# RMSNorm on one core: scaling shared between VectorE and GpSimd, squares on ScalarE, and a fixed instruction order

## The chip, the cores and the metric

The kernel runs on one core of one Trainium2 chip. The metric is the time on the device of one execution, in microseconds (us); a time quoted for a kernel is the median of its runs. The profiler's span of one execution is a little shorter than that time: 160.0 us for the kernel before, whose time in the same set of runs is about 162 us.

## The reference

The input is 16 x 1024 rows of 512 float32 values; gamma has 512 values.

```python
def reference(x, gamma):
    eps = 1e-5
    rms = np.sqrt(np.mean(x ** 2, axis=-1, keepdims=True) + eps)
    return (x / rms * gamma).astype(np.float32)
```

The work per row is a sum of squares, a root, a reciprocal and two multiplications. The input and the output are 33.55 MB each, so 67.1 MB have to be moved.

## The kernel before

The 16,384 rows are cut into four tiles of 128 partitions x 32 rows. Three buffers (slots) in SBUF, the core's memory for tiles, hold a tile each; rows are scaled in place and stored from there. Tile 3 goes into slot 0 again, so it can be loaded only after tile 0 has been stored. A "row" below is one row of 512 values on each of 128 partitions, so the core has 128 of them.

```python
def row_stats(slot, g):                      # 8 rows; gives 1/rms
    ...
    if (g // G) % 2:                         # every second group:
        for h in range(0, G, H):             # ScalarE squares 4 rows at once,
            nc.scalar.activation(out=sq, in_=slots[slot][:, g + h : g + h + H, :], func=AF.Square)
            nc.vector.tensor_reduce(...)     # VectorE sums them
    else:
        for r in range(G):                   # ScalarE squares and sums a row
            nc.scalar.activation(out=sq_scratch, ..., func=AF.Square, accum_out=ss[:, r : r + 1])
    nc.scalar.activation(out=rms, in_=ss, func=AF.Sqrt, ...)
    nc.vector.reciprocal(out=rstd, in_=rms)

def apply(slot, g, rstd):                    # VectorE scales all rows
    for r in range(G):
        nc.vector.scalar_tensor_tensor(..., scalar=rstd[:, r : r + 1], in1=gamma_b, ...)

def transfers(t, g):                         # all of them issued by SyncE, in this order
    if (t, g) == (0, 0):
        store(0, 0, 0, 1)                    # tile 0, slot 0, row 0
        load(1, 1, 0, 32)                    # all of tile 1
        load(2, 2, 0, 16)
        store(0, 0, 1, 2)
        load(2, 2, 16, 32)
    ...

ahead = row_stats(0, 0)
for k, (t, g) in enumerate(groups):
    rstd = ahead
    if k + 1 < len(groups):
        ahead = row_stats(slot_of[tn], gn)   # the next group's statistics,
    apply(slot_of[t], g, rstd)               # then this group's scaling
    transfers(t, g)
```

The loads of tiles 1 and 2 stand, in SyncE's order, behind the store of row 0. And although the program text has the next group's statistics ahead of this group's scaling, the order on each engine is chosen here by a scheduler.

## Time and profile before

| | before |
|---|---|
| time, median of 3 runs | 162.24 us (161.93 to 162.32) |
| span | 160.0 us |
| DMA queue q1, share of the span | 97.9% |
| VectorE busy | 122.6 us (77%) |
| ScalarE busy | 80.1 us (50%) |
| GpSimd busy | 0.2 us |

These are lines of the page of the kernel before. DVE is VectorE, ACT is ScalarE, POOL is GpSimd. The row DMA has one digit for each fortieth of the span (4 us): the busy share of the 16 DMA engines in tenths, 9 for 90% or more. The row GB/s has what they moved.

```profile
span 160.0 us, 409 instructions
...
PE 2.0 (1%) x2; PEld 0.5 (0%) x2; DVE 122.6 (77%) x163; ACT 80.1 (50%) x162; POOL 0.2 (0%) x4
...
DMA  5999999699699999997999999999996996999993
GB/s 197 524 393 393 430 487 508 279 524 491 295 395 396 456 467 434 494 461 323 445 393 475 426 410 426 475 410 410 491 524 295 508 491 295 467 434 410 426 475 147
...
q1 hardware_dynamic: 2160, 67.11, 97.9%
```

The DMA engines are busy from the first slice to the last, and no compute engine is. The windows view of the same kernel, with longer stretches, takes the jitter of the slices out. Its columns are the stretch, its length, the busy time and instructions of PE, PEld, DVE, ACT and POOL, the clock, the DMA share and GB/s. (A packet is counted where it is recorded, so a short stretch can show a little over 1.00.)

```profile
22.00:34.00 12.00, 0.00 (x0) 0.00 (x0) 9.23 (x8) 11.12 (x16) 0.00 (x0) 1.00 1.07 459
34.00:116.00 82.00, 0.00 (x0) 0.00 (x0) 76.61 (x105) 50.34 (x107) 0.00 (x0) 1.00 1.00 431
...
124.00:158.00 34.00, 0.00 (x0) 0.00 (x0) 22.59 (x32) 6.29 (x15) 0.00 (x0) 1.00 1.00 432
158.00:162.00 4.00, 0.00 (x0) 0.00 (x0) 0.00 (x0) 0.00 (x0) 0.00 (x0) 1.00 0.00 0
```

The queue moves 431 to 432 GB/s wherever it is full. The Trainium skill, "DMA: Bandwidth & Descriptors", section Specifications, gives a ceiling of 435 GB/s for the ports between the DMA engines and SBUF, and this trace, loads and stores together, agrees. So the kernel is bound by its transfers, and a faster compute engine has next to nothing to win.

The timeline of the kernel before around the first store has start, length, engine, line and operation. SPq is SyncE's sequencer, which issues the transfers.

```profile
15.55 0.20 DVE L83 RECIPROCAL rstd<-rms 128x8 f32<-128x8 f32 x1 [10.61 <-ACT rms L82]
15.79 3.40 DVE L88 SCALAR_TENSOR_TENSOR slot<-slot,rstd,gamma_b 128x512 f32<-128x512 f32 x5
16.57 0.35 SPq L45 DMA_DIRECT2D out_dram<-slot  x1
16.97 0.92 SPq L42 DMA_DIRECT2D slot<-in_x_dram  x2
```

VectorE scales row 0 straight after its reciprocal. The store goes out at 16.57 us and the loads of tiles 1 and 2 from 16.97 us, while tile 0 is still being loaded. These two groups of instructions give the cost of VectorE's work (busy us in total, mean ns of one):

```profile
L88 DVE SCALAR_TENSOR_TENSOR slot<-slot,rstd,gamma_b 128x512 f32<-128x512 f32 x128 | 85.8, 741 | 0.1
...
L71 DVE TENSOR_REDUCE ss<-sq 128x4 f32<-128x2048 f32 x16 | 35.9, 2277 | 3.6 <-ACT sq L70 3.6
```

### The profile page before, as it was taken

What the parts mean: (1) busy time and instruction counts of PE and PEld (TensorE: products, weight loads), DVE (VectorE), ACT (ScalarE), POOL (GpSimd) and SP (SyncE); (2) the same over time, 40 slices, a digit from 0 to 9 for tenths busy, and PEclk for the clock granted to TensorE, in tenths of its full rate; (3) what the DMA queues carried; (4) which work ended last, traced back from release to release, by engine and by line L of the source; (5) the groups of instructions that cost most, each with busy time, mean ns of one, the idle gap of its engine ahead of it and who ended that gap; (6) DMA issues with size and microseconds to landing.
All of it is one profiled execution on the core that took longest, in us unless ns stands there. A gap on an engine that the chain in (4) does not pass through costs nothing.

```text
span 160.0 us, 409 instructions
## 1 busy us (share of the span) xinstructions
PE 2.0 (1%) x2; PEld 0.5 (0%) x2; DVE 122.6 (77%) x163; ACT 80.1 (50%) x162; POOL 0.2 (0%) x4
## 2 busy tenths in 40 slices
PE   4000000000000000000000000000000000000000
PEld 1000000000000000000000000000000000000000
DVE  0101928999999509999999999999999999996000
ACT  3098029991291999996900960069709950000000
POOL 0000000000000000000000000000000000000000
DMA  5999999699699999997999999999996996999993
GB/s 197 524 393 393 430 487 508 279 524 491 295 395 396 456 467 434 494 461 323 445 393 475 426 410 426 475 410 410 491 524 295 508 491 295 467 434 410 426 475 147
DMA packets 2164, 67.13 MB, mean 420 GB/s; under 512 B 241, under 2 KB 241, under 8 KB 498
## 3 DMA queue, kind: packets, MB, share of 16 engines
q1 hardware_dynamic: 2160, 67.11, 97.9%
q14 instruction: 2, 0.02, 0.0%
q10 hardware_dynamic: 2, 0.00, 0.0%
HBM read 33.56 MB, written 33.55 MB: 419 GB/s over the span
## 4 chain that ended last, share of the span: by engine, by line
DVE 67%; DMA 14%; ACT 7%; issue 2%; DVEq 0%; SPq 0%
DVE slot L88 48%; DVE ss L71 18%; DMA slot<-in_x_dram 14%; ACT sq_scratch L76 3%; ACT sq L70 3%; DVE rstd L83 1%; ACT rms L82 1%; DVEq L155 0%; SPq L42 0%
## 5 line engine op out<-in xcount | busy, mean ns | idle before, releaser
L88 DVE SCALAR_TENSOR_TENSOR slot<-slot,rstd,gamma_b 128x512 f32<-128x512 f32 x128 | 85.8, 741 | 0.1
L76 ACT ACTIVATE sq_scratch<-slot 128x512 f32<-128x512 f32 x64 | 40.0, 625 | 10.0 <-DMA slot<-in_x_dram 8.7
L70 ACT ACTIVATE sq<-slot 128x2048 f32<-128x2048 f32 x16 | 29.8, 1865 | 18.8 <-DVE ss L71 11.5
L71 DVE TENSOR_REDUCE ss<-sq 128x4 f32<-128x2048 f32 x16 | 35.9, 2277 | 3.6 <-ACT sq L70 3.6
L82 ACT ACTIVATE rms<-ss,eps_t 128x8 f32<-128x8 f32 x16 | 4.6, 297 | 26.2 <-DVE ss L71 26.0
L83 DVE RECIPROCAL rstd<-rms 128x8 f32<-128x8 f32 x16 | 3.1, 196 | 16.3 <-ACT rms L82 16.3
L76 ACT ACTIVATION_READ_ACCUMULATOR sq_scratch<-slot 128x1 f32 x64 | 11.9, 186 | 0.0
L57 DVE COPY gamma_b<-sq 128x512 f32<-128x512 f32 x1 | 0.7, 691 | 3.3 <-PE sq L55 3.3
L55 PE MATMUL sq<-gamma_row,ones_col 1*128 1x512 f32 x2 | 2.0, 1122 | 2.2 <-DMA gamma_row<-in_gamma_dram 2.2
L76 ACT ACT_TABLE_LOAD x1 | 1.3, 1283 | 1.3 <-PEq L144 1.3
L82 ACT ACT_TABLE_LOAD x1 | 1.3, 1283 | 0.0
L53 DVE MEMSET ones_col<- 1x128 f32 x1 | 0.2, 165 | 0.8 <-PEq L144 0.8
L55 PEld LDWEIGHTS sq<-gamma_row,ones_col 1*128 1x128 f32 x2 | 0.5, 308 | 2.1 <-issue 2.1
L144 POOL MEMSET const-uint8-127<- 128x1 uint8 x1 | 0.1, 102 | 0.0
L144 POOL MEMSET const-bfloat16-1.0<- 128x1 bf16 x1 | 0.1, 101 | 0.0
L144 POOL MEMSET const-float32-0.0<- 128x1 f32 x1 | 0.1, 98 | 0.2 <-issue 0.2
L144 POOL MEMSET const-float32-1.0<- 128x1 f32 x1 | 0.1, 98 | 0.0
L60 DVE MEMSET eps_t<- 128x1 f32 x1 | 0.1, 59 | 0.0
## 6 DMA issues: line engine op xcount, KB each, us to landing
slot<-in_x_dram SPq DMA_DIRECT2D x4, 4096.0 KB, 32.1
out_dram<-slot SPq DMA_DIRECT2D x4, 4096.0 KB, 18.4
out_dram<-slot SPq DMA_DIRECT2D x1, 7680.0 KB
slot<-in_x_dram SPq DMA_DIRECT2D x1, 6144.0 KB, 21.6
slot<-in_x_dram SPq DMA_DIRECT2D x1, 2048.0 KB, 7.2
out_dram<-slot SPq DMA_DIRECT2D x2, 256.0 KB, 21.4
gamma_row<-in_gamma_dram ACTq DMA_DIRECT2D x1, 2.0 KB
slot<-in_x_dram SPq DMA_DIRECT2D x1, 25.9
```

Source lines behind the costliest of these rows:

```text
L53: nc.vector.memset(ones_col, 1.0)
L55: nc.tensor.matmul(gamma_psum[:, 0], ones_col, gamma_row, start=True, stop=True)
L57: nc.vector.tensor_copy(out=gamma_b, in_=gamma_psum[:, 0])
L60: nc.vector.memset(eps_t, eps)
L70: nc.scalar.activation(out=sq, in_=slots[slot][:, g + h : g + h + H, :], func=AF.Square)
L71: nc.vector.tensor_reduce(out=ss[:, h : h + H], in_=sq, axis=mybir.AxisListType.X, op=OP.add)
L76: nc.scalar.activation(out=sq_scratch, in_=slots[slot][:, g + r, :], func=AF.Square, accum_out=ss[:, r : r + 1],)
L82: nc.scalar.activation(out=rms, in_=ss, func=AF.Sqrt, bias=eps_t, scale=1.0 / D)
L83: nc.vector.reciprocal(out=rstd, in_=rms)
L88: nc.vector.scalar_tensor_tensor(out=slots[slot][:, g + r, :], in0=slots[slot][:, g + r, :], scalar=rstd[:, r : r + 1], in1=gamma_b, op0=O ...
L144: nc = _bacc.Bacc("TRN2", target_bir_lowering=False, num_devices=1)
```

## The change

The intent is to share the compute out better. ScalarE only squares, several rows at once. VectorE sums all rows, but scales only 80 of 128; GpSimd scales the other 48 in two passes, by 1/rms and by gamma. VectorE reads gamma from PSUM, the memory that a matmul writes to, and no longer from SBUF. The order is fixed as the program has it, VectorE's code is aligned (`addr_align(128)`), and the last tile is loaded ahead of the store of tile 1, the second one. The core of the diff:

```diff
+    ctx.enter_context(tc.manual_schedule())
+    nc.vector.addr_align(128, offset=0, max_nops=0)
...
+    groups = [                       # tile, first row, rows, pieces, GpSimd's rows
+        (0, 0, 8, (4, 4), 3),
+        (0, 8, 12, (7, 5), 5),
+        (0, 20, 12, (7, 5), 5),
+        (1, 0, 16, (7, 5, 4), 7),
...
+    def sum_squares(t, g, n, pieces, share):
...
+            nc.scalar.activation(out=sq[:, :m], in_=rows, func=AF.Square)
+            nc.vector.tensor_reduce(out=ss[:, r : r + m], in_=sq[:, :m], ...)
...
+    def scale_by_pool(rstd, t, g, n, pieces, share):
+        part = slots[slot_of[t]][:, g + n - share : g + n, :]
+        by_row = rstd[:, n - share : n].to_broadcast([P, share, D])
+        nc.gpsimd.tensor_tensor(out=part, in0=part, in1=by_row, op=OP.mult)
+        nc.gpsimd.tensor_tensor(out=part, in0=part, in1=gamma_b.to_broadcast([P, share, D]), op=OP.mult)
...
     def transfers(t, g):             # (0, 0) is as it was
-        elif (t, g) == (0, 24):
-            store(0, 0, 2, 32)
-        elif (t, g) == (1, 8):
-            store(1, 1, 0, 16)
+        elif (t, g) == (0, 20):
+            store(0, 0, 2, 16)
+            store(0, 0, 16, 32)
             load(3, 0, 0, 16)
             load(3, 0, 16, 32)
-        elif (t, g) == (1, 24):
-            store(1, 1, 16, 32)
+        elif (t, g) == (1, 16):
+            store(1, 1, 0, 32)
...
+    rstd = inverse_rms(sum_squares(*groups[0]), groups[0][2])
+    for k, group in enumerate(groups):
+        t, g, n, pieces, share = group
+        scale_by_pool(rstd, *group)
+        following = groups[k + 1 :][:1]
+        for nxt in following:
+            ss = sum_squares(*nxt)            # the next group's squares and sums
+        for r in range(n - share):
+            scale_row(rstd, t, g, r)          # and only then this group's scaling
+            if r == 2:
+                for nxt in following:
+                    rstd_next = inverse_rms(ss, nxt[2])
+        rstd = rstd_next
         transfers(t, g)
```

More of the change, by code (lines that the diff above doesn't have):

```diff
@@ L27 @@
     R = 32
-    G = 8
-    H = 4
     assert N == 4 * P * R
@@ L33 @@
     ov = of.rearrange("(t p r) d -> t p r d", p=P, r=R)
+    ctx.enter_context(tc.manual_schedule())
+    nc.vector.addr_align(128, offset=0, max_nops=0)
     const = ctx.enter_context(tc.tile_pool(name="const", bufs=1))
     stats = ctx.enter_context(tc.tile_pool(name="stats", bufs=4))
-    psum = ctx.enter_context(tc.tile_pool(name="psum", bufs=2, space=bass.MemoryType.PSUM))
+    psum = ctx.enter_context(tc.tile_pool(name="psum", bufs=1, space=bass.MemoryType.PSUM))
     slots = [const.tile([P, R, D], fp32, name=f"slot{i}") for i in range(3)]
@@ L52 @@
     ones_col = const.tile([1, P], fp32)
-    nc.vector.memset(ones_col, 1.0)
-    gamma_psum = psum.tile([P, H, D], fp32, name="sq")
-    nc.tensor.matmul(gamma_psum[:, 0], ones_col, gamma_row, start=True, stop=True)
-    gamma_b = const.tile([P, D], fp32)
-    nc.vector.tensor_copy(out=gamma_b, in_=gamma_psum[:, 0])
-    eps_t = const.tile([P, 1], fp32)
-    nc.vector.memset(eps_t, eps)
-    sq_scratch = const.tile([P, D], fp32)
-    def row_stats(slot, g):
-        ss = stats.tile([P, G], fp32, name="ss")
-        rms = stats.tile([P, G], fp32, name="rms")
-        rstd = stats.tile([P, G], fp32, name="rstd")
-        if (g // G) % 2:
-            for h in range(0, G, H):
-                sq = psum.tile([P, H, D], fp32, name="sq")
-                nc.scalar.activation(out=sq, in_=slots[slot][:, g + h : g + h + H, :], func=AF.Square)
-                nc.vector.tensor_reduce(
-                    out=ss[:, h : h + H], in_=sq, axis=mybir.AxisListType.X, op=OP.add
-                )
-        else:
-            for r in range(G):
-                nc.scalar.activation(
-                    out=sq_scratch,
-                    in_=slots[slot][:, g + r, :],
-                    func=AF.Square,
-                    accum_out=ss[:, r : r + 1],
-                )
-        nc.scalar.activation(out=rms, in_=ss, func=AF.Sqrt, bias=eps_t, scale=1.0 / D)
-        nc.vector.reciprocal(out=rstd, in_=rms)
-        return rstd
@@ L86, in apply @@
-    def apply(slot, g, rstd):
-        for r in range(G):
-            nc.vector.scalar_tensor_tensor(
-                out=slots[slot][:, g + r, :],
-                in0=slots[slot][:, g + r, :],
-                scalar=rstd[:, r : r + 1],
-                in1=gamma_b,
-                op0=OP.mult,
-                op1=OP.mult,
-            )
-    groups = [(t, g) for t in range(4) for g in range(0, R, G)]
-    slot_of = [0, 1, 2, 0]
+    nc.gpsimd.memset(ones_col, 1.0)
+    gamma_psum = psum.tile([P, D], fp32, name="gamma_psum")
@@ new lines @@
+    nc.tensor.matmul(gamma_psum, ones_col, gamma_row, start=True, stop=True)
+    gamma_b = const.tile([P, 1, D], fp32)
+    nc.scalar.copy(out=gamma_b[:, 0], in_=gamma_psum)
+    eps_t = const.tile([P, 1], fp32)
+    nc.gpsimd.memset(eps_t, eps)
+    groups = [
[3 more added lines that the diff above has]
+        (1, 0, 16, (7, 5, 4), 7),
+        (1, 16, 16, (7, 5, 4), 7),
+        (2, 0, 16, (7, 5, 4), 6),
+        (2, 16, 16, (7, 5, 4), 6),
+        (3, 0, 16, (7, 5, 4), 6),
+        (3, 16, 16, (7, 5, 4), 3),
+    ]
@@ new lines @@
+    slot_of = [0, 1, 2, 0]
+    def sum_squares(t, g, n, pieces, share):
+        ss = stats.tile([P, 16], fp32, name="ss")
+        r = 0
+        for k, m in enumerate(pieces):
+            if k % 2:
+                sq = const.tile([P, 5, D], fp32, name="sq_sbuf")
+            else:
+                sq = psum.tile([P, 7, D], fp32, name="sq_psum")
+            rows = slots[slot_of[t]][:, g + r : g + r + m, :]
+            nc.scalar.activation(out=sq[:, :m], in_=rows, func=AF.Square)
+            nc.vector.tensor_reduce(
+                out=ss[:, r : r + m], in_=sq[:, :m], axis=mybir.AxisListType.X, op=OP.add
+            )
+            r += m
+        return ss
@@ new lines, in inverse_rms @@
+    def inverse_rms(ss, n):
+        rms = stats.tile([P, 16], fp32, name="rms")
+        rstd = stats.tile([P, 16, 1], fp32, name="rstd")
+        nc.scalar.activation(out=rms[:, :n], in_=ss[:, :n], func=AF.Sqrt, bias=eps_t, scale=1.0 / D)
+        nc.vector.reciprocal(out=rstd[:, :n, 0], in_=rms[:, :n])
+        return rstd
+    def scale_by_pool(rstd, t, g, n, pieces, share):
[3 more added lines that the diff above has]
+        nc.gpsimd.tensor_tensor(out=part, in0=part, in1=gamma_b.to_broadcast([P, share, D]), op=OP.mult)
@@ L100, in transfers, with scale_row @@
+    def scale_row(rstd, t, g, r):
+        x = slots[slot_of[t]][:, g + r, :]
+        nc.vector.scalar_tensor_tensor(
+            out=x, in0=x, scalar=rstd[:, r], in1=gamma_psum, op0=OP.mult, op1=OP.mult
+        )
     def transfers(t, g):
@@ L106, in transfers @@
             load(2, 2, 16, 32)
-        elif (t, g) == (0, 24):
-            store(0, 0, 2, 32)
-        elif (t, g) == (1, 8):
-            store(1, 1, 0, 16)
+        elif (t, g) == (0, 20):
+            store(0, 0, 2, 16)
+            store(0, 0, 16, 32)
             load(3, 0, 0, 16)
             load(3, 0, 16, 32)
-        elif (t, g) == (1, 24):
-            store(1, 1, 16, 32)
-        elif (t, g) == (2, 24):
+        elif (t, g) == (1, 16):
+            store(1, 1, 0, 32)
+        elif (t, g) == (2, 16):
             store(2, 2, 0, 32)
-        elif (t, g) == (3, 8):
+        elif (t, g) == (3, 0):
             store(3, 0, 0, 16)
-        elif (t, g) == (3, 24):
+        elif (t, g) == (3, 16):
             store(3, 0, 16, 32)
-    ahead = row_stats(0, 0)
-    for k, (t, g) in enumerate(groups):
-        rstd = ahead
-        if k + 1 < len(groups):
-            tn, gn = groups[k + 1]
-            ahead = row_stats(slot_of[tn], gn)
-        apply(slot_of[t], g, rstd)
+    rstd = inverse_rms(sum_squares(*groups[0]), groups[0][2])
[11 more added lines that the diff above has]
+        rstd = rstd_next
         transfers(t, g)
```

## The prediction

> **What bounds the kernel now.** The DMA engines. The page of the kernel before gives queue q1 97.9% of the span; the windows view has 432 GB/s at a DMA share of 1.00 from 3 to 157.6 us. 67.1 MB at 431 GB/s is 155.7 us; with about 2.2 us before the first packet and 2.1 after the last, the span is 160.0 us. The Trainium skill, "DMA: Bandwidth & Descriptors", section Bandwidth, gives a 435 GB/s ceiling; the trace agrees. VectorE is busy 122.6 us (77%), ScalarE 80.1, GpSimd 0. So no change of compute can gain more than about 1%, and a wait that empties the queue costs its full length.
>
> **What the change does to engines.** VectorE: all 128 rows are reduced from squares (64 before: 2277 ns per 4 rows), 80 rows scaled instead of 128 (741 ns each, about 660 apart in the chain). In chain spacing: 70 us of reductions (8.7 per 16 rows) plus 53 of scaling: about 125 us, no relief. ScalarE drops to about 60 us (fit to 625 ns for one row, 1865 for four: 3.1 us for seven). GpSimd gets 48 rows, twice each. No trace shows that operation; an estimate from the skill, "GPSIMD Engine Reference", section Performance versus the Vector engine (4497 ns for 2048 elements), is 108 us. Aligning VectorE's code saves at most the issue gaps in the chain of waits (1.5, 0.5, 0.5, 0.7 us), off the limit.
>
> **What the fixed order does.** SyncE issues in order, and the loads of tiles 1 and 2 stand behind the store of row 0. Before, VectorE scaled group 0 straight after its reciprocal; the store went out at 16.57 us and the loads at 16.97, before tile 0's load ran dry (about 21.6 us). In the built order of the changed kernel VectorE goes reciprocal, reduce 7 rows, reduce 5 rows of the next group, only then row 0; by the semaphore counts, the store waits for that row. The next group's rows land at 22.8 us (timeline, before). So: squares to 25.9, reductions to 32.4, row 0 to 33.1, tile 1's load issued at 33.5, flowing at 35. The queue is empty from 21.6 to 35: **13 us lost**, all on the critical path, since 58.7 MB (136 us) remain.
>
> A second, small gap: after tile 1 lands (about 56), VectorE has 80 rows to reduce and 45 to scale before tile 2 is complete, about 133 us, while tile 1's store ends at 132.4: 2 to 3 us more. If GpSimd needs over about 2.4 ns per element, this gap grows. The reordered last load neither gains nor loses: no gap stood there before.
>
> **Predicted.** Queue end about 174, span 176, time 178 us (161.8 for a span of 160.0 in the profiled run); 8 in 10 between 174 and 186. Faster by over 2%: 0.02; within 2%: 0.03; slower by over 2%: 0.95.
>
> **Right or wrong in the profile.** (1) The 40-slice DMA row shows about 13 us of zeros near 22 to 35 us. (2) The first store and tile 1's load are issued at 33 us, SyncE waiting on VectorE's scaling. (3) The rate outside the gaps is still 425 to 435 GB/s. (4) VectorE busy 122 to 132 us, ScalarE about 60, GpSimd 100 to 125. (5) A gap of 2 to 8 us before tile 2's store, near 132.
>
> **What would make it wrong.** GpSimd well over 2.6 ns per element, or VectorE slowed by it: over 186. Row 0 scaled before the next reductions on the chip, against the built order: near 162. Gamma read from PSUM costing more per row: each 65 ns adds about 3 us to the second gap.

## The result and the profile after

| | before | after |
|---|---|---|
| time, median | 162.18 us (161.93 to 162.32, 4 runs) | 176.0 us (175.83 to 177.33, 4 runs) |
| span of the profiled run | 160.0 us | 174.2 us |
| ratio of times, after to before | | 1.087 (95% interval 1.082 to 1.093) |

The kernel is 8.7% slower. Ratios here and below are the mean time of one kernel's fast runs over that of the other's of the same rounds, so they are not quite the ratio of the medians that are quoted. The output is correct.

The page of the kernel after, the same lines:

```profile
span 174.2 us, 275 instructions
...
PE 2.0 (1%) x2; PEld 0.5 (0%) x2; DVE 123.6 (71%) x113; ACT 63.6 (36%) x36; POOL 96.5 (55%) x24
...
DMA  6998800099699999999999899999979996989995
GB/s 217 448 530 372 361 0 0 27 514 451 286 466 421 421 368 482 414 417 428 450 391 466 376 481 444 399 481 481 436 331 436 481 451 271 481 361 481 421 421 241
...
q1 hardware_dynamic: 2160, 67.11, 90.6%
```

The DMA row now has three zeros; a slice is 4.4 us here, so they stand for 21.8 to 34.8 us. VectorE's busy time has hardly changed, 123.6 us against 122.6. The windows view of the kernel after:

```profile
22.00:34.00 12.00, 0.00 (x0) 0.00 (x0) 7.63 (x4) 6.40 (x4) 1.28 (x1) 1.00 0.00 0
34.00:116.00 82.00, 0.00 (x0) 0.00 (x0) 70.34 (x64) 39.74 (x21) 62.65 (x11) 1.00 1.00 422
...
116.00:133.00 17.00, 0.00 (x0) 0.00 (x0) 17.00 (x18) 8.10 (x5) 13.60 (x3) 1.00 1.00 432
133.00:136.00 3.00, 0.00 (x0) 0.00 (x0) 3.00 (x1) 0.00 (x0) 2.92 (x2) 1.00 0.82 350
```

From 22 to 34 us the queue moved nothing, where it moved 459 GB/s before. After that it is nearly as fast as before, apart from a small dip at 133 us: 425 GB/s from 34.5 to 116 us by the windows view (the line above begins half a microsecond before the first packet), and 432 from 116 to 133 us. The timeline of the kernel after shows why (the last lines are of the later stretch):

```profile
23.18 3.16 ACT L86 ACTIVATE sq_psum<-slot 128x3584 f32<-128x3584 f32 x1 [6.45 <-DMA slot<-in_x_dram]
...
26.37 3.89 DVE L87 TENSOR_REDUCE ss<-sq_psum 128x7 f32<-128x3584 f32 x1 [9.41 <-ACT sq_psum L86]
30.18 2.81 DVE L87 TENSOR_REDUCE ss<-sq_sbuf 128x5 f32<-128x2560 f32 x1
32.90 2.05 DVE L108 SCALAR_TENSOR_TENSOR slot<-slot,rstd,gamma_psum 128x512 f32<-128x512 f32 x3
...
33.67 0.35 SPq L46 DMA_DIRECT2D out_dram<-slot  x1
34.07 0.42 SPq L43 DMA_DIRECT2D slot<-in_x_dram  x1
...
133.06 0.34 SPq L46 DMA_DIRECT2D out_dram<-slot  x1
```

VectorE stood idle for 9.41 us, waiting for squares of rows that had only just landed, summed them, and only then, at 32.90 us, scaled row 0, whose 1/rms had long been there. The store of row 0 went out at 33.67 us instead of 16.57, and the loads behind it at 34.07 us instead of 16.97. Tile 0's load was over at about 23 us. Between, the queue had nothing to do.

The single DMA packets in the trace give the sizes. No packet at all was under way for 11.8 us, from 22.7 to 34.5 us. Averaged over the 16 engines, and with the edges where some of them have run dry, that gap cost 12.7 us. The dip near 133 us, where tile 2's store waited for VectorE, cost 0.6 us. The packets themselves took 1.25 us longer in all, 157.9 against 156.7 us of each engine's time. These three sum to 14.6 us, and the span grew by 14.2 us. The difference lies at the end: in the kernel before, the engines end within 1.0 us of each other, which costs 0.6 us by the same count, and in the kernel after they end together (0.1 us).

The groups of the kernel after, by form, show the new work on VectorE and GpSimd:

```profile
L108 DVE SCALAR_TENSOR_TENSOR slot<-slot,rstd,gamma_psum 128x512 f32<-128x512 f32 x80 | 53.2, 724 | 0.0
...
L104 POOL TENSOR_TENSOR slot<-slot,gamma_b 128x3072 f32<-128x3072 f32 x3 | 20.0, 6666 | 0.2
L103 POOL TENSOR_TENSOR slot<-slot,rstd 128x3072 f32<-128x3072 f32 x3 | 15.9, 5310 | 6.2 <-DVE rstd L97 6.2
```

A GpSimd multiplication took 1.73 ns per element by 1/rms (5310/3072) and 2.17 by gamma (6666/3072).

### The profile page after: what moved, and what is told of

The parts are those of the page before. It is cut to its first block, busy times and chain, and to the rows that moved or that the text cites. A ratio compares the mean times of both kernels' runs of the same rounds, so it can differ in the third digit from the quotient of the medians.

```text
span 174.2 us, 275 instructions
## 1 busy us (share of the span) xinstructions
PE 2.0 (1%) x2; PEld 0.5 (0%) x2; DVE 123.6 (71%) x113; ACT 63.6 (36%) x36; POOL 96.5 (55%) x24
## 4 chain that ended last, share of the span: by engine, by line
DVE 57%; DMA 25%; ACT 4%; issue 3%; SPq 0%; DVEq 0%
DVE ss L87 32%; DMA slot<-in_x_dram 25%; DVE slot L108 25%; ACT sq_psum L86 4%; DVE rstd L97 1%; DVEq L172 0%; SPq L43 0%; SPq L46 0%
## 5 line engine op out<-in xcount | busy, mean ns | idle before, releaser
L103 POOL TENSOR_TENSOR slot<-slot,rstd 128x3072 f32<-128x3072 f32 (+3 forms) x9 | 42.7, 4741 | 52.4 <-DVE rstd L97 52.4
L87 DVE TENSOR_REDUCE ss<-sq_psum 128x7 f32<-128x3584 f32 (+1 forms) x15 | 47.0, 3131 | 31.6 <-ACT sq_psum L86 31.6
L86 ACT ACTIVATE sq_psum<-slot 128x3584 f32<-128x3584 f32 (+1 forms) x15 | 38.3, 2556 | 45.3 <-DVE ss L87 22.7
L104 POOL TENSOR_TENSOR slot<-slot,gamma_b 128x3072 f32<-128x3072 f32 (+3 forms) x9 | 53.5, 5949 | 0.7
L108 DVE SCALAR_TENSOR_TENSOR slot<-slot,rstd,gamma_psum 128x512 f32<-128x512 f32 x80 | 53.2, 724 | 0.0
L87 DVE TENSOR_REDUCE ss<-sq_sbuf 128x5 f32<-128x2560 f32 (+1 forms) x9 | 24.7, 2744 | 0.0
L86 ACT ACTIVATE sq_sbuf<-slot 128x2560 f32<-128x2560 f32 (+1 forms) x9 | 20.5, 2274 | 0.0
L96 ACT ACTIVATE rms<-ss,eps_t 128x16 f32<-128x16 f32 (+2 forms) x9 | 2.8, 306 | 27.1 <-DVE ss L87 27.1
L97 DVE RECIPROCAL rstd<-rms 128x16 f32<-128x16 f32 (+2 forms) x9 | 2.1, 229 | 1.7 <-ACT rms L96 1.7
L56 PE MATMUL gamma_psum<-gamma_row,ones_col 1*128 1x512 f32 x2 | 2.0, 1122 | 2.5 <-DMA gamma_row<-in_gamma_dram 2.5
```

Source lines behind the costliest of these rows:

```text
L56: nc.tensor.matmul(gamma_psum, ones_col, gamma_row, start=True, stop=True)
L86: nc.scalar.activation(out=sq[:, :m], in_=rows, func=AF.Square)
L87: nc.vector.tensor_reduce(out=ss[:, r : r + m], in_=sq[:, :m], axis=mybir.AxisListType.X, op=OP.add)
L96: nc.scalar.activation(out=rms[:, :n], in_=ss[:, :n], func=AF.Sqrt, bias=eps_t, scale=1.0 / D)
L97: nc.vector.reciprocal(out=rstd[:, :n, 0], in_=rms[:, :n])
L103: nc.gpsimd.tensor_tensor(out=part, in0=part, in1=by_row, op=OP.mult)
```

## The experiments

The theory: the fixed order put row 0's scaling behind sums whose rows were still in flight; the store of row 0 waited for it, and the loads of tiles 1 and 2 waited behind that store. This held-back load is the main loss, and a second, small shortage comes from tile 2 being finished late. The rivals are: the new division of work costs the time (GpSimd too slow, or GpSimd and VectorE in each other's way), or the reordered transfers cost it; and VectorE's own idle time near 20 us costs it, whatever the loads do. (Where an expectation names a theory by a letter, A is the first of these and C the last.)

Medians of the kernel before were 161.76, 161.92, 161.89 and 161.96 us, each on the same chip as the kernels compared with it. All kernels gave a correct result.

### e1: row 0 scaled first

The changed kernel, with the first group scaled before the next group's sums.

```diff
+        early = n - share if k == 0 else 0
+        for r in range(early):
+            scale_row(rstd, t, g, r)
         for nxt in following:
             ss = sum_squares(*nxt)
-        for r in range(n - share):
+            if early:
+                rstd_next = inverse_rms(ss, nxt[2])
+        for r in range(early, n - share):
             scale_row(rstd, t, g, r)
```

> The changed kernel, except that VectorE scales its five rows of the first group before it reduces the next group's rows. Theory A (the gate): the loads of tiles 1 and 2 wait in SyncE's order for row 0, which the fixed order puts behind rows that land only at 23 us. Then the first store leaves at about 17.6 us, the empty stretch of 11.8 us goes, and 162.8 to 165 us remain: a small shortage before tile 2's store (about 2 us) stays, because VectorE's work after tile 1's landing and the transfers move forward together. Rival B (the new work itself: GpSimd beside VectorE, or slower transfers): it keeps most of the loss, 172 us or more.

Measured: 164.82 us (164.6 to 164.96), ratio to before 1.018 (1.016 to 1.020), span 163.3 us; within the expectation. The timeline of e1, transfers only:

```profile
17.73 0.35 SPq L46 DMA_DIRECT2D out_dram<-slot  x1
18.13 0.91 SPq L43 DMA_DIRECT2D slot<-in_x_dram  x2
```

The store and the loads are out in time. The change cost 13.8 us (176.0 less 162.18). With nothing but the place of five scalings in the order changed, 3.1 us are left (164.82 less 161.76, the kernel before in the same rounds), so 10.8 are gone. GpSimd, the sums on VectorE, gamma in PSUM and the reordered load were all still there. The windows view of e1 shows where the rest is:

```profile
116.00:124.00 8.00, 0.00 (x0) 0.00 (x0) 8.00 (x12) 5.07 (x2) 6.29 (x2) 1.00 0.63 270
```

With the first gap gone, the queue reaches tile 2's store earlier than VectorE has finished tile 2: VectorE is busy for all 8 us, and the queue at 0.63. By the packets this shortage cost 3.4 us.

### e2: loads first

The changed kernel with its order kept, but the loads taken from behind the store.

```diff
     load(0, 0, 8, 32)
+    load(1, 1, 0, 32)
+    load(2, 2, 0, 16)
+    load(2, 2, 16, 32)
...
             store(0, 0, 0, 1)
-            load(1, 1, 0, 32)
-            load(2, 2, 0, 16)
             store(0, 0, 1, 2)
-            load(2, 2, 16, 32)
```

> The changed kernel with every engine's order as it is, except SyncE's: the loads of tiles 1 and 2 are issued at the start, ahead of the store of row 0. Theory A: the queue never runs dry at 22 us although row 0 is still scaled at 33 us; 163 to 166 us, at most 1.5 us over the run with row 0 first. If it is instead VectorE's own idling in that stretch that costs (rival C: VectorE is the limit, with 124 us busy and idle until 26 us), VectorE's idle time is not shortened by this and most of the loss stays, 172 us or more.

Measured: 164.29 us (164.14 to 164.42), ratio 1.015 (1.013 to 1.017), span 162.8 us; within the expectation. The timeline of e2, transfers only (and one line of a later stretch):

```profile
0.73 2.37 SPq L43 DMA_DIRECT2D slot<-in_x_dram  x5
33.90 27.84 SPq L46 DMA_DIRECT2D out_dram<-slot  x4
...
121.61 0.34 SPq L46 DMA_DIRECT2D out_dram<-slot  x1
```

The store of row 0 is as late as ever, 33.90 us, and VectorE waits as before. Still only 2.5 us of the 13.8 are left (164.29 less 161.76), so 11.3 are gone, because the loads no longer stand behind that store. So it was the loads behind the store that cost the time. The late store and VectorE's idle time can have cost at most the 2.5 us by which e2 is still slower than the kernel before. The remaining shortage, 2.5 us by the packets, is again the one before tile 2's store, issued at 121.61 us.

### e3: the kernel before, in fixed order

The converse: the kernel before with one added line, and none of the rest of the change.

```diff
+    ctx.enter_context(tc.manual_schedule())
     const = ctx.enter_context(tc.tile_pool(name="const", bufs=1))
```

> The kernel before, with one line added: its instructions keep the order of the program text. No work moves to GpSimd, ScalarE still sums half of the rows, no reordered load. Its text also sums the next group before it scales the present one. Theory A: the first store leaves at about 31 us and not at 17, the queue is empty for 9 to 11 us, and the time is 171 to 177 us: the order alone makes the loss. Rival B: within 2% of the kernel before (159 to 165).

Measured: 176.0 us (175.93 to 176.07), ratio 1.087 (1.085 to 1.089), span 174.3 us. The timeline of e3, transfers only, and its windows view:

```profile
30.21 0.35 SPq L46 DMA_DIRECT2D out_dram<-slot  x1
30.60 0.93 SPq L43 DMA_DIRECT2D slot<-in_x_dram  x2
```

```profile
24.00:31.00 7.00, 0.00 (x0) 0.00 (x0) 6.16 (x6) 4.18 (x8) 0.00 (x0) 1.00 0.00 0
```

One line makes the same kind of gap, with no scaling on GpSimd in the kernel at all. The queue is empty for 8.9 us, a little less than the 9 to 11 that were expected. That the total is 176.0 us as well is partly a coincidence: the fixed order made two more shortages in this kernel, by the packets 1.6 us near 130 and 2.9 near 160 us. The time was expected right, but it was a shorter first gap and more trouble later.

### e4: the kernel before, last tile loaded ahead

```diff
         elif (t, g) == (0, 24):
-            store(0, 0, 2, 32)
-        elif (t, g) == (1, 8):
-            store(1, 1, 0, 16)
+            store(0, 0, 2, 16)
+            store(0, 0, 16, 32)
             load(3, 0, 0, 16)
             load(3, 0, 16, 32)
         elif (t, g) == (1, 24):
-            store(1, 1, 16, 32)
+            store(1, 1, 0, 32)
```

> The kernel before, with only the transfers reordered as in the change: tile 0 stored as rows 2 to 16 and 16 to 32, tile 3 loaded ahead of tile 1's store, tile 1 stored whole. Theory A: no gap stood there before, so the same time within 0.7% (161 to 163.3). If the reordering were a gain that the gate hides, it would be under 160.5; if it were part of the loss, over 164.

Measured: 161.95 us (161.85 to 162.5), ratio 1.001 (0.999 to 1.004). The reordered transfers neither gain nor lose, as predicted.

### e5: ScalarE sums some rows again

The kernel e2, with ScalarE squaring and summing the last four rows of each group of tiles 1 and 2, to take the second shortage away. (To make room in SBUF, the gamma row shares memory with the scratch.)

```diff
+            if k == 2 and t in (1, 2):
+                for i in range(m):
+                    nc.scalar.activation(
+                        out=sq_scratch, in_=rows[:, i], func=AF.Square, accum_out=ss[:, r + i : r + i + 1]
+                    )
+                continue
             nc.scalar.activation(out=sq[:, :m], in_=rows, func=AF.Square)
```

> The run with the loads first, and besides, in tiles 1 and 2, ScalarE squares and sums the last four rows of each group itself (as the kernel before does), so VectorE has 16 rows fewer to reduce, 8.8 us, before tile 2 is complete. Theory A: the remaining 2.5 us over the kernel before are the queue waiting for tile 2, which VectorE completes at 121.5 us while tile 1's store ends near 119; with VectorE done near 113 that wait goes, and the time is 161.3 to 162.8 us. Rival (GpSimd's traffic or the order of transfers slows the queue): stays at 163.8 or more.

Measured: 163.62 us (163.13 to 164.03), ratio 1.010 (1.007 to 1.013), span 162.0 us. The expectation was missed by 0.8 us, and the time lies between its range and the rival's. The shortage went, as the timeline of e5 (tile 2's store) and its windows view show, but the time fell by only about a third of what was left (ratio 1.010, against 1.015 in e2):

```profile
112.77 0.34 SPq L46 DMA_DIRECT2D out_dram<-slot  x1
```

```profile
116.00:124.00 8.00, 0.00 (x0) 0.00 (x0) 8.00 (x8) 2.19 (x2) 5.09 (x2) 1.00 0.91 393
...
158.00:162.00 4.00, 0.00 (x0) 0.00 (x0) 0.00 (x0) 0.00 (x0) 0.00 (x0) 1.00 0.04 16
```

Tile 2's store is issued 8.8 us earlier than in e2, and the packets show no shortage in the middle. In place of it there is a tail: 16 GB/s at a share of 0.04 after 158 us, where the kernel before has 0. The packets say the same: those of all engines but one end between 156.3 and 157.1 us after the first packet, and then two more follow, one at a time, the last of them ending 2.0 us later. One engine of the 16 still works while the others are done. (That it is one engine is read from the packets following one another; the records do not name it.)

### e6: more rows for GpSimd

The kernel e2, with 8 instead of 7 rows of each group of tile 1 on GpSimd.

```diff
-        (1, 0, 16, (7, 5, 4), 7),
-        (1, 16, 16, (7, 5, 4), 7),
+        (1, 0, 16, (7, 5, 4), 8),
+        (1, 16, 16, (7, 5, 4), 8),
```

> The run with the loads first, with GpSimd's share raised from 7 to 8 rows in both groups of tile 1. VectorE saves two scalings, 1.3 us, before tile 2 is complete; GpSimd gets 4 us more and completes its part of tile 2 near 118 us, still ahead of VectorE. Theory A: 1.0 to 1.5 us less than the 164.3 us of the run with the loads first: 162.8 to 163.4. If GpSimd is what tile 2 waits for, it gets longer by 2 to 4 us instead: over 166.

Measured: 163.8 us (162.95 to 163.91), ratio 1.010 (1.007 to 1.013). The median is 0.4 us above the upper end, so the size was missed; the direction is as expected. Less work on VectorE and more on GpSimd made the kernel a little faster than e2 (its ratio was 1.015, 1.013 to 1.017; the two intervals only just part, and the chips differed), and the packets show the shortage before tile 2's store at 1.1 us instead of 2.5. At the end, one engine is 1.0 us behind the others here too. GpSimd is not the limit there; VectorE is.

### e7: without the alignment

```diff
-    nc.vector.addr_align(128, offset=0, max_nops=0)
```

> The changed kernel without the alignment of VectorE's code. Theory A: it touches only issue gaps of at most 0.7 us on VectorE; 175.5 to 177.5 us. If the alignment carried weight, over 178.

Measured: 175.44 us (175.25 to 176.22), ratio 1.085 (1.082 to 1.088), 0.06 us below the lower end of the expectation. The interval overlaps that of the changed kernel (1.082 to 1.093): the alignment has no effect on the time that these runs can show. The issue gaps that it might have closed are still in the changed kernel's chain of waits, one of 1.52 us at 28.66 us.

### e8: no rows for GpSimd

The kernel e2, with every share set to 0 and the GpSimd scaling taken out.

```diff
-        (0, 0, 8, (4, 4), 3),
+        (0, 0, 8, (4, 4), 0),
...
-        scale_by_pool(rstd, *group)
```

> The run with the loads first, with GpSimd's share set to nothing: VectorE scales all 128 rows. Theory A: GpSimd relieves VectorE of 39 rows (26 us) before tile 2 is complete, and without it VectorE, not the queue, sets the end: 186 to 194 us, GpSimd busy under 1 us, VectorE about 155. VectorE's scaling should take the same 724 ns a row: if GpSimd slows VectorE, it drops below 700 here, and the time is under 184.

Measured: 190.53 us (one run), span 188.8 us; within the expectation. The page and the groups of e8:

```profile
PE 2.0 (1%) x2; PEld 0.5 (0%) x2; DVE 155.0 (82%) x161; ACT 63.5 (34%) x36; POOL 0.4 (0%) x6
```

```profile
L111 DVE SCALAR_TENSOR_TENSOR slot<-slot,rstd,gamma_psum 128x512 f32<-128x512 f32 x128 | 84.9, 734 | 0.0
```

A scaling took 734 ns on VectorE without GpSimd at work, and 724 with it (in the changed kernel). So GpSimd did not slow VectorE. With ScalarE doing no sums, VectorE needs GpSimd's help: taking it away cost 26 us. The division of work is thus a trade among the compute engines. It gives GpSimd what VectorE had to take over from ScalarE, and leaves VectorE where it was.

### e9: gamma in SBUF

The kernel e2, with VectorE reading gamma from SBUF, as the kernel before does.

```diff
-            out=x, in0=x, scalar=rstd[:, r], in1=gamma_psum, op0=OP.mult, op1=OP.mult
+            out=x, in0=x, scalar=rstd[:, r], in1=gamma_b[:, 0], op0=OP.mult, op1=OP.mult
```

> The run with the loads first (164.3 us), with one operand changed: VectorE's scaling reads gamma from the copy in SBUF that GpSimd also reads, and no longer from PSUM. If VectorE's second SBUF input and GpSimd exclude each other for whole instructions, as the Trainium skill says of the shared port, VectorE's scalings wait up to 8 us for a GpSimd operation to end: scalings with waits or durations of several us, and a time of 172 us or more. If they share, the scaling stays at 720 to 745 ns and the time under 166.

Measured: 240.93 us (one run), span 239.3 us; as expected. The same group in e2 and in e9, and a stretch of e9's timeline:

```profile
L111 DVE SCALAR_TENSOR_TENSOR slot<-slot,rstd,gamma_psum 128x512 f32<-128x512 f32 x80 | 53.3, 729 | 0.0
...
L111 DVE SCALAR_TENSOR_TENSOR slot<-slot,rstd,gamma_b 128x512 f32<-128x512 f32 x80 | 134.0, 1737 | 0.0
```

```profile
72.27 16.02 DVE L111 SCALAR_TENSOR_TENSOR slot<-slot,rstd,gamma_b 128x512 f32<-128x512 f32 x4
72.42 6.52 POOL L106 TENSOR_TENSOR slot<-slot,rstd 128x3584 f32<-128x3584 f32 x1 [12.16 <-DVE rstd L100]
...
79.02 8.06 POOL L107 TENSOR_TENSOR slot<-slot,gamma_b 128x3584 f32<-128x3584 f32 x1
```

Four scalings, about 3 us of work, took 16.02 us, while GpSimd's two instructions ran. The Trainium skill, "SBUF — State Buffer", section Who interferes with whom (the passage that the expectation means), says that a VectorE instruction with two inputs in SBUF and a GpSimd instruction that reads SBUF exclude each other for a whole instruction. By the same section, a VectorE instruction with at most one SBUF input, outside certain fast modes, does not contend with GpSimd. Both halves are seen here: a mean of 1737 ns with gamma in SBUF, and 729 in e2, which differs only in gamma's place. Moving gamma to PSUM is what makes the change's division of work possible here.

### e10: row 0 first, and ScalarE's sums

The edits of e1 and of the sums in e5 together, to see whether the tail in e5 comes from its early loads. Five rounds.

```diff
+        early = n - share if k == 0 else 0
...
+            if k == 2 and t in (1, 2):
+                for i in range(m):
+                    nc.scalar.activation(..., accum_out=ss[:, r + i : r + i + 1])
+                continue
```

> The run with row 0 first, with ScalarE summing the last four rows of each group in tiles 1 and 2. It keeps the one-row stores apart from each other, among the loads, as the kernel before has them; in the run with loads first and these sums, they stood together behind the loads, the rate fell to 390 GB/s from 58 to 66 us (447 in the kernel before), and 1.7 us over the kernel before remained with no wait for tile 2. If those stores are the rest, this run has 161.5 to 162.9 us; if not, 163.2 or more again.

Measured: 163.95 us (163.43 to 164.34), ratio 1.012 (1.010 to 1.015). The hoped-for range was missed. The end of the span is as in e5, to the digit: 16 GB/s at a share of 0.04 from 158 to 162 us. By the packets, one engine ends 2.3 us behind the others. The early loads are not its cause, and neither is the order of the first loads and stores.

### e11: no one-row stores

The kernel e5 without the two stores of a single row. Five rounds.

```diff
-            store(0, 0, 0, 1)
-            store(0, 0, 1, 2)
+            pass
...
-            store(0, 0, 2, 16)
+            store(0, 0, 0, 16)
```

> The run with the loads first and ScalarE's sums (163.6 us), without the two one-row stores: rows 0 and 1 go out with rows 2 to 16 in one store. If the small stores cost what remains, 161.0 to 162.5 us, no slower than the kernel before and perhaps up to 0.6% faster; if the remainder is of another kind (one of the 16 DMA engines behind the rest at the end), 163 or more.

Measured: 164.34 us (163.75 to 164.62), ratio 1.014 (1.012 to 1.017). Missed again, with the same tail. The small stores are not its cause.

### e12: the kernel before, loads first

The kernel before with the edit of e2. Five rounds.

```diff
     load(0, 0, 8, 32)
+    load(1, 1, 0, 32)
+    load(2, 2, 0, 16)
+    load(2, 2, 16, 32)
...
             store(0, 0, 0, 1)
-            load(1, 1, 0, 32)
-            load(2, 2, 0, 16)
             store(0, 0, 1, 2)
-            load(2, 2, 16, 32)
```

> The kernel before with the loads of tiles 1 and 2 issued at the start, so that no load stands behind a store; VectorE's order is the same, instruction by instruction. Theory A: its queue never ran dry, so the gate was worth nothing there: 161.3 to 162.8 us, within 0.6% of the kernel before. If instead the order of the transfers is what leaves 2 us in the three mended versions of the changed kernel (at the end 16 GB/s from 158 us on, one of 16 DMA engines still busy), this run shows that too: 163.3 us or more.

Measured: 162.38 us (162.33 to 162.64), ratio 1.003 (1.002 to 1.005), span 160.6 us; within the expectation. The windows view of e12:

```profile
158.00:162.00 4.00, 0.00 (x0) 0.00 (x0) 0.00 (x0) 0.00 (x0) 0.00 (x0) 1.00 0.02 8
```

In the kernel before, the order of loads and store costs nothing, since row 0 is ready in time. Taking the loads out from behind the store even costs 0.3%, and a small tail shows here too.

No version beat the kernel before. The best repaired versions of the change, e5 and e6, are 1.0% slower, because the queue was full all along and compute had nothing to give. What stays open is the tail of some 2 us in e5, e10 and e11, in which a single DMA engine still works. It is not the order of the first loads (e10 has the old one), nor the small stores (e11 has none), nor the reordered last load by itself (e4 has it, and its engines end within 0.9 us). Why one engine lags was not found.

When it lags can be read from the kept traces. Each transfer ends with sixteen packets of 4 bytes (240 for the 15 transfers), taken here as one from each engine. In e5 the last of the sixteen comes 0.8 us after the fifteenth at the first load already, and 2.0 us after it in each transfer from the one that ends at 102.9 us to the last. In e2 the lag is 2.0 us too, up to the transfer that ends at 122 us; after the shortage it is 0.03 us. In e1 it falls from 2.3 to 0.02 us, and in e6, whose shortage is 1.1 us, from 2.0 to 1.0 us. In the kernel before it is never over 0.4 us. So a shortage gives the lagging engine time to catch up, and taking the shortage away brings the lag to light. This accounts for the small gain of e5: e2's shortage had covered a lag of 2.0 us that was there already.

## Why the prediction was right

The prediction was 178.0 us, with a range of 174 to 186, and 0.95 for slower by over 2%. Measured were 176.0 us. Point by point:

- **The limit.** Right: the queue moved 431 to 432 GB/s when full before, and 425 to 432 after, and none of the twelve versions came below the kernel before. (The prediction's margins were off: the packets begin 1.7 us after the start, not 2.2, and end 1.2 us before the end of the span, not 2.1.)
- **The held-back loads.** Right, and shown from both sides: e1 and e2 undo it in two ways and take off 10.8 and 11.3 of 13.8 us; e3 makes it in the kernel before with one line. Row 0's store was predicted for about 33.1 us and went out at 33.67; tile 1's load for 33.5, and it went out at 34.07.
- **The size of that gap.** Predicted: empty from 21.6 to 35 us, 13 us. Measured: from 22.7 to 34.5, 11.8 us with no packet at all. The start was set too early, since tile 0's last packets were under way until 22.7 us. Counted over the 16 engines with the ragged edges, the gap cost 12.7 us.
- **The second shortage.** The place and the cause were right: tile 2's store was predicted for about 133 us and issued at 133.06. The size was not. The prediction's step "2 to 3 us more" is the term that was mis-sized: 0.6 us by the packets. It was a difference of two large sums, VectorE's finish less the end of tile 1's store, and so the small error of each went into it whole. Slower packets, 1.25 us, which the prediction did not have, made up for part of it; why they were slower was not looked into. That e1 and e2 show this shortage at 3.4 and 2.5 us, once the first gap no longer delays the queue, fits the same account: the first gap put off the moment at which the queue needed tile 2, and so hid most of this shortage. That last step is argued from the numbers, and no run varied it alone.
- **The engines.** VectorE 123.6 us busy (122 to 132 predicted) and ScalarE 63.6 (about 60) were right. GpSimd was 96.5 us, under the predicted 100 to 125. The estimate of 108 us came from the Trainium skill, "GPSIMD Engine Reference", section Performance versus the Vector engine, 4497 ns for an addition of 2048 elements, which is 2.20 ns each. The trace agrees for the multiplication by gamma (2.17), and differs for that by 1/rms (1.73). It had no weight in the time, as e6 shows.
- **The reordered load and the alignment.** No effect predicted beyond noise; e4 and e7 agree.
- **Contention.** The prediction named VectorE slowed by GpSimd as a thing that could make it wrong. It did not happen, 724 ns for a scaling against 741 before, because gamma lies in PSUM; e9 shows what would have come otherwise.

## What to carry to other kernels

In a fixed order, work that waits for data still in flight must not stand ahead of work that is ready and that releases a transfer; and a load should not be issued behind a store that waits for compute, unless that store is sure to be ready first. When the DMA queue is full from start to end, look first at what a change does to the times at which transfers are issued, for dividing compute anew had nothing to win there, and all the time for which a late issue leaves the queue empty is lost (here the loads were issued 17.1 us later, and the queue was empty for 11.8). A wait that is taken away can bring another to light that it had covered, as the lagging engine in e5 shows. When VectorE and GpSimd scale side by side, keep VectorE's second operand out of SBUF.

## What the Trainium skill lacked or had wrong

- "DMA: Bandwidth & Descriptors", section Anatomy of one DMA: it says that a wait for a semaphore happens on the sequencer that issues the transfer. The section does not draw the consequence: a waiting store holds back every later transfer of that sequencer. Here loads issued 17.1 us later (34.07 against 16.97) left the queue empty for 11.8 us.
- The same page, section Bandwidth, Where 436 GB/s comes from: it says that for transfers between HBM and SBUF the HBM side, about 358 GB/s, binds. With one core at work the queue moved 432 GB/s. The same section says just before that a single core's figures are higher, so the two statements should be joined there, as other pages of the skill join them.
- "GPSIMD Engine Reference", section Performance versus the Vector engine: one measured time, for an addition of two tensors, 4497 ns for 2048 elements (2.20 ns each), and none for a second operand that is repeated. The runs show 1.73 ns where the second operand is one value per row, and 2.17 ns where it is a row of 512 that is repeated.
- "SBUF — State Buffer", section Who interferes with whom: the rule was confirmed. For who is held up, the page goes by the order of issue; it does not have what comes of that when short VectorE instructions run in turn with long GpSimd ones. In e9 a scaling took up to 8208 ns instead of about 700, and GpSimd's instructions grew only from 6.17 to 6.52 and from 7.76 to 8.06 us.
- "DMA: Bandwidth & Descriptors", section Latency and other measured facts: it has two of the engines, 7 and 15, as usually slower in traces, with a guess at the cause that it limits to transfers issued by GpSimd. Here SyncE issues them, and one engine (the records do not say which) ended some 2 us behind the rest in e5, e10 and e11. The page does not say how far behind an engine can fall, that it catches up when the queue runs short (from 2.0 us to 0.03 in e2), or what decides it.
